# The opening of a two-layer backbone kernel, up to group 0's first eight tiles, issued in written order on four engines

## The chip, the cores and the metric

The kernel runs on one core of a Trainium2 chip. The metric is device time in microseconds (us) of one launch. The engines are PE (TensorE, matrix multiply), DVE (VectorE), ACT (ScalarE), POOL (GpSimd) and SP (SyncE, which here issues all loads).

## The reference, cut to what matters

Four mixers exist; two layers are run, so only the pooling mixer (layer 0) and the neighbourhood attention (layer 1) occur. What follows is layer 0, on 256 latent and 256 context tokens of width 2048:

```
ml = (silu(c) @ w_mod[i] + b_mod[i]).reshape(B, 6, 1, D)       # 6 x 2048 modulation values, and the same for c_ctx
a  = rms_norm(h, norm1_g) * (1 + scale) + shift                # ml[:,1], ml[:,0]
h  = h + ml[:, 2] * pool_mix(a, pool_w, pool_b, pool_scale)    # 4 groups of 512 channels, windows 2/4/8/16
u  = rms_norm(h, norm2_g) * (1 + ml[:, 4]) + ml[:, 3]
h  = h + ml[:, 5] * conv_ffn(u, w_gate, w_up, ...)             # 2048 -> 5504 (gate, up) -> 2048
```

`pool_mix` takes a windowed mean minus the token itself, and multiplies each group of 512 channels by its own 512 x 512 matrix.

## The kernel before, in words

All products that need single precision are made of three fast ones: a weight and an activation are split into a high part (a cast on ACT, line 152 for weights) and a low part (a subtraction on DVE, line 155), and hi x hi, hi x lo and lo x hi are added up in PSUM.

The 24 chunks of 512 modulation values are made in **modulation steps** (`mod_pe`, line 189; matmuls at line 197). A chunk has four steps. One step loads 1 MB of `w_mod` in two loads of 512 KB and multiplies it in four column blocks of 32, two blocks from each load; line 197 has eight PE instructions for a step and four for a half. After the fourth step of a chunk comes its finish: ACT copies the sum out (line 204), PE transposes it four times (line 209), DVE reduces it and adds bias and gain (lines 213, 178, 180). The generator `pump0` runs steps in the order of chunks 4, 0, 8, 16, 12, and then two at a time; `need(n)` advances it to step n.

Layer 0's mixer and the first half of its feed-forward are interleaved by groups of 512 channels. `mixer(0)` (from line 627) makes the pooled values of group 0 (`pfs`), scales them by chunk 4 (line 663), shifts them by chunk 0 (line 664), splits them (`parts_of`, lines 614 and 615), multiplies them by `wp[0]` into four banks `pm0_0` to `pm0_3` (`pool_mm`, lines 623, 624, 626), scales the result by chunk 8 (`gsc`, `gbi`, lines 691 and 693; 707 and 710) and adds it to the streams `hl` and `hc` (line 712). Then it scales these by chunk 16 into the split operands `Ad` (lines 722, 723). `partial(0)` multiplies `Ad` by the first eight blocks of `w_gate` and `w_up`: a **tile** is twelve matmuls (lines 787 to 789) into one bank, four tiles come from one pair of loads (`wcg`, `wcu`), and each sum is copied out (line 799). `early_shifts` (line 743) multiplies the same raw weight loads by chunk 12, which DVE has copied into `sh` (line 573).

Loads go to 15 **rooms** of 512 KB that are used in turn (`stage`, line 117): six in the pool `wst` and the unused operand rooms A7 to A15 (nine, given by `lend`). A room is free again when the last instruction that reads it is done.

The order of instructions on each engine is chosen by the framework's planner, which goes by the order of the code, by what its own plan says is ready, and by a few marks: `tc.high_priority()`, `tc.issue_after(ins)`. So two halves of one step can stand apart on PE, with other matmuls between them, and a load can be issued ahead of an earlier one whose room isn't free.

Of the kernel before, what the change touches and what calls it, by code (L numbers as in the profile page):

```python
# [17 lines left out]
P = 128  # L18
D = 2048
KT = D // P  # L20
T = 256
# [39 lines left out]
def kernel(ctx: ExitStack, tc: tile.TileContext, xT, cxT, wmod, wg, wu, wd, wp,  # L61
# [20 lines left out]


# [26 lines left out]
    made = []  # L110
    first_split = []
# [28 lines left out]
    def split(ts, name, share=0, lows=None):  # L140

        parts = []
        for j, (t, n) in enumerate(ts):
# [5 lines left out]
            with ExitStack() as behind:  # L149
                for ins in hold:  # L150
                    behind.enter_context(tc.issue_after(ins))
                cast = nc.scalar.copy(hi[:, :n], t[:, :n])  # L152
                eng = nc.gpsimd if share and turn[0] % share == 0 else nc.vector
                if lows is None:
                    low = eng.tensor_tensor(lo[:, :n], t[:, :n], hi[:, :n].bitcast(F32), op=ALU.subtract)  # L155
                    made[:] = [cast.ins, low.ins]
                else:
                    lows.append((lo, t, hi))
# [27 lines left out]
    def behind(ch, j):  # L186
        return tc.issue_after(first_split[j]) if ch == 16 else ExitStack()

    def mod_pe(chs, sc, pool):

        ps = bank("m", f"mod{chs[0]}")
        for c, ch in enumerate(chs):
            for g in range(4):
# [7 lines left out]
                if ch == chs[-1] and g == 3:  # L201
                    ev = pool.tile([P, 512], F32, tag="t2", name=f"modev{ch}")
                    with tc.high_priority() if ch in (0, 4, 8, 16) else ExitStack(), behind(ch, 0):
                        copied[ch] = nc.scalar.copy(ev, ps).ins
                yield
        with tc.high_priority() if ch in (0, 4, 8, 16) else ExitStack():
# [3 lines left out]
            for c, ch in enumerate(chs):  # L210
                r = main.tile([P, 4, 2], F32, name=f"modT0_{ch}")
                with behind(ch, 1):
                    nc.vector.tensor_reduce(out=r, in_=by_row(p2, 2 * c), axis=AX.X, op=ALU.add)
                finish_mod(0, ch, r)

# [258 lines left out]
    with ExitStack() as ph0:  # L474
# [58 lines left out]
        with ExitStack() as phs:  # L533
# [50 lines left out]
            def need(n):  # L584
                while done[0] < n:
                    next(pump0, None)
                    done[0] += 1
# [40 lines left out]
            def mixer(g):  # L628
# [8 lines left out]
                if g == 0:  # L637
# [19 lines left out]
                    parts = split(load(lambda a, b: wp[0][:, a:b], 2048, "wp0"), "wp0", lows=lows)  # L657
                    yield
                    for k in range(4):
                        for s in both:  # L660
                            v = pfs[k][:, s, :]
                            with tc.issue_after(copied[0]) if k > 1 else ExitStack():
                                nc.scalar.activation(v, v, AF.Copy, scale=M(0, 1, k, s))
                            nc.vector.scalar_tensor_tensor(v, z, M(0, 0, k, s), v, op0=ALU.mult, op1=ALU.add)
# [4 lines left out]
                    yield  # L669
# [21 lines left out]
                nc.vector.tensor_tensor(gsc, modT[0, 8 + g].rearrange("p i s -> p (i s)"), V("ps")[:, 8 * g : 8 * g + 8],  # L691
                                        op=ALU.mult)
                nc.vector.tensor_tensor(gbi, gsc, V("pb")[:, 8 * g : 8 * g + 8], op=ALU.mult)
                for m in range(4):
                    if banks:
                        ps = banks[m]
                    else:
                        ps = bank("d", f"pm{g}_{m}")
                        for i in range(4):
                            pool_mm(ps, parts, pa, i, m)  # L700
                    k = 4 * g + m
                    y = f0.tile([P, 2, T], F32, tag="t2", name=f"pz{k}")
                    for s in both:
                        j = 2 * m + s
                        v = ps[:, T * s : T * s + T]
                        if g == 0 and s == 0:
                            nc.vector.tensor_scalar(y[:, s], v, gsc[:, j : j + 1], gbi[:, j : j + 1],
                                                    op0=ALU.mult, op1=ALU.add)
                        else:
                            nc.scalar.activation(y[:, s], v, AF.Identity, scale=gsc[:, j : j + 1], bias=gbi[:, j : j + 1])  # L710
                        eng = nc.vector if g == 0 and s == 0 else nc.gpsimd
                        eng.tensor_tensor(h_of(s)[:, k, :], h_of(s)[:, k, :], y[:, s], op=ALU.add)
                    if g:
                        n2.add(h_of, k)
# [3 lines left out]
                for i in range(4):  # L718
# [8 lines left out]
                    if i == 1:  # L727
# [25 lines left out]

            def partial(g, sh, between):
# [3 lines left out]
                for fa in range(0, NS, 4):  # L758
                    for q, (nm, wsrc) in enumerate((("g", wg), ("u", wu))):
                        if step:  # L760
                            ahead.clear()
                        if ahead:
                            ts, parts = ahead
                        else:
                            ts = load(lambda a, b: wsrc[0, fa + a // 512 : fa + b // 512, :, 512 * g : 512 * g + 512]
                                      .rearrange("f p c -> p f c"), 2048, f"wc{nm}{g}_{fa}")
                            parts = split(ts, f"wc{nm}{g}_{fa}")
                        for j in range(4):
# [14 lines left out]
                            hi, lo = parts[j // 2]  # L783
                            for i in range(4):
                                o = 512 * (j % 2) + P * i
                                xh, xl = flat(A[4 * g + i][:, 0]), flat(A[4 * g + i][:, 1])
                                nc.tensor.matmul(ps, hi[:, o : o + P], xh, start=(first and i == 0), stop=False)
                                nc.tensor.matmul(ps, hi[:, o : o + P], xl, start=False, stop=False)
                                ins = nc.tensor.matmul(ps, lo[:, o : o + P], xh, start=False, stop=(final and i == 3))
                                if i == 1:  # L790
                                    between(2 * step + 1)
                            step += 1
                            first_tile.append(ins.ins)
                            if f >= NC:
                                continue
                            if g == 0:
                                if q == 0:
                                    PART[f] = act_tile(f"part{f}", F32)
                                nc.scalar.copy(PART[f][:, q], ps)
                            else:  # L800
                                ins = nc.vector.tensor_tensor(PART[f][:, q], PART[f][:, q], ps, op=ALU.add)
                                if g == 3:
                                    added.append(ins.ins)
# [11 lines left out]
            first_tile = []  # L815
            first = mix = mixer(0)
            for n in (0, 8, 11, 13, 13, 17, 17):
                if n == 17 and not ahead:
                    need(15)
                    ahead.append(load(lambda a, b: wg[0, 0:2, :, 0:512].rearrange("f p c -> p f c"), 1024, "wcg0_0"))  # L820
                    ahead.append(split(ahead[0], "wcg0_0"))
                    first_split[:] = made
# [785 lines left out]
```

## Time and profile before

| | us |
|---|---|
| median of 3 runs (lowest, highest) | 3010.19 (3008.44, 3012.23) |
| the profiled execution, its own time | 3006.95 |
| span of the profile | 3005.2 |
| PE busy in the span | 2954.4 (98%) |
| DVE, ACT, POOL busy | 2035.4, 1353.9, 876.8 |

Times in the profile count from the start of the span. A matmul's end is modelled, so pitches between starts say more than durations. "xN" is a number of instructions; the bracket behind a row is the idle time before it on its engine and what ended it.

### The profile page before, as it was taken

Reading aid. Unit: us, or ns where it says so; the run is one execution under the profiler, and the core shown is the slowest. Engines: PE = TensorE matmul, PEld = TensorE weight load, DVE = VectorE, ACT = ScalarE, POOL = GpSimd, SP = SyncE. Lnnn points to the kernel's source line nnn. Section 1 sums busy time; section 2 is a strip of 40 time slices with the busy share of each in tenths; the row PEclk is TensorE's granted clock in tenths of the full one; section 3 lists DMA queues with packets and bytes.
Section 4 is the critical chain, followed back from the end, with each engine's and each line's share of the span. In section 5 each row is a group of like instructions: output and inputs, shape, how many; then the busy total and the mean of one; then the engine's idle time right before and its main releaser. Section 6 shows DMA issues by size and latency. Waiting matters only on the chain.

```text
span 3005.2 us, 41071 instructions
## 1 busy us (share of the span) xinstructions
PE 2954.4 (98%) x14922; PEld 2402.8 (80%) x14922; DVE 2035.4 (68%) x2908; ACT 1353.9 (45%) x2225; POOL 876.8 (29%) x864
## 2 busy tenths in 40 slices
PE   7999999999999999999999999999999999999998
PEld 3655678888888888888887888888888888888887
DVE  5455887666786867688777656474877666666666
ACT  3333573323333233333434434353556666566665
POOL 1011310312214031231422111020101565566665
PEclk9999999999999999999999999999999999999999
DMA  9988535555876867786782333333356565555553
GB/s 390 344 297 324 198 99 177 166 174 169 247 209 185 269 181 234 211 246 192 229 242 85 123 107 113 97 118 95 118 165 207 170 203 194 189 180 187 185 187 113
DMA packets 224923, 572.32 MB, mean 190 GB/s; under 512 B 55248, under 2 KB 68304, under 8 KB 224720
## 3 DMA queue, kind: packets, MB, share of 16 engines
q1 hardware_dynamic: 224720, 569.70, 58.6%
q8 instruction: 117, 1.92, 0.3%
q14 instruction: 86, 0.70, 0.1%
HBM read 563.32 MB, written 11.53 MB: 191 GB/s over the span
## 4 chain that ended last, share of the span: by engine, by line
PE 93%; DVE 3%; DMA 2%; ACT 1%; issue 1%; POOL 0%; SPq 0%; DVEq 0%; ACTq 0%; POOLq 0%
PE g L1102 5%; PE u L1102 5%; PE d L950 5%; PE d L952 5%; PE d L951 5%; PE d L1174 5%; PE u L915 4%; PE u L913 4%; PE u L914 4%; PE g L915 4%; PE g L914 4%; PE g L913 4%; PE u L1109 3%; PE g L1109 3%; PE d L1178 3%; PE mod L197 2%
## 5 line engine op out<-in xcount | busy, mean ns | idle before, releaser
L971 POOL TENSOR_TENSOR hl<-hl,dy 128x256 f32<-128x256 f32 x144 | 148.7, 1033 | 921.4 <-ACT dy L968 662.2
L1191 POOL TENSOR_TENSOR hl<-hl,dy 128x256 f32<-128x256 f32 x320 | 313.6, 1011 | 231.6 <-ACT dy L1189 228.7
L284 DVE SCALAR_TENSOR_TENSOR macc<-wm,sc,macc 128x512 f32<-128x512 f32 x360 | 262.8, 780 | 7.7 <-DMA wm<-wmod 7.4
L262 DVE SCALAR_TENSOR_TENSOR macc<-wm,sc,macc 128x1024 f32<-128x1024 f32 x120 | 161.3, 1344 | 91.9 <-DMA wm<-wmod 90.9
L968 ACT ACTIVATE dy<-d,modT 128x256 f32<-128x256 f32 x224 | 93.2, 470 | 121.0 <-PE d L952 114.9
L971 POOL TENSOR_TENSOR hc<-hc,dy 128x256 f32<-128x256 f32 x144 | 141.8, 985 | 0.0
L1372 POOL COPY bias<-rows 128x160 f32<-128x160 f32 x64 | 39.7, 631 | 312.7 <-DVE nm L1381 234.5
L1189 ACT ACTIVATE dy<-d,modT 128x512 f32<-128x512 f32 x160 | 104.6, 684 | 57.1 <-PE d L1178 55.5
L155 DVE TENSOR_TENSOR wd_3l<-wd,wd_3h 128x1024 fp32r<-128x1024 f32 (+1 forms) x44 | 56.0, 1278 | 79.6 <-ACT wd_3h L152 79.0
L517 ACT ACTIVATE sg<-g 128x512 f32<-128x512 f32 x43 | 27.3, 634 | 160.1 <-DVE g L514 160.0
L197 PE MATMUL mod<-wm,sc 128*32 128x512 f32 x640 | 95.3, 606 | 3.1 <-DMA wm<-wmod 2.9
L155 DVE TENSOR_TENSOR wd_2l<-wd,wd_2h 128x1024 fp32r<-128x1024 f32 (+1 forms) x44 | 58.2, 1333 | 41.9 <-ACT wd_2h L152 41.4
L607 POOL TENSOR_TENSOR pf<-ws,inv 128x256 f32<-128x256 f32 x32 | 29.3, 937 | 195.8 <-DVE ws L599 86.2
L155 DVE TENSOR_TENSOR wd_1l<-wd,wd_1h 128x1024 fp32r<-128x1024 f32 (+1 forms) x44 | 55.2, 1259 | 36.7 <-ACT wd_1h L152 36.7
L152 ACT CAST wd_0h<-wd 128x1024 fp32r<-128x1024 f32 (+1 forms) x44 | 45.2, 1031 | 57.9 <-PE g L914 41.1
L152 ACT CAST wd_1h<-wd 128x1024 fp32r<-128x1024 f32 (+1 forms) x44 | 44.9, 1029 | 51.8 <-PE u L1102 28.8
L950 PE MATMUL d<-act,wd_0h 128*128 128x512 f32 x172 | 66.4, 390 | 1.0 <-ACT dy L968 1.0
L950 PE MATMUL d<-act,wd_3h 128*128 128x512 f32 x172 | 67.2, 391 | 0.0
L952 PE MATMUL d<-act,wd_2l 128*128 128x512 f32 x172 | 67.2, 390 | 0.0
L951 PE MATMUL d<-act,wd_2h 128*128 128x512 f32 x172 | 67.1, 390 | 0.0
L950 PE MATMUL d<-act,wd_2h 128*128 128x512 f32 x172 | 66.9, 389 | 0.0
L952 PE MATMUL d<-act,wd_0l 128*128 128x512 f32 x172 | 66.9, 389 | 0.0
(1710 smaller groups left out, 9319.6 us busy)
## 6 DMA issues: line engine op xcount, KB each, us to landing
wm<-wmod SPq DMA_DIRECT2D x384, 512.0 KB, 6.2
wd<-wd SPq DMA_DIRECT2D x168, 512.0 KB, 4.4
wg<-wg SPq DMA_DIRECT2D x156, 512.0 KB, 4.5
wu<-wu SPq DMA_DIRECT2D x156, 512.0 KB, 4.7
wv<-wv SPq DMA_DIRECT2D x32, 512.0 KB, 3.9
wk<-wq SPq DMA_DIRECT2D x32, 512.0 KB, 3.8
wq<-wq SPq DMA_DIRECT2D x32, 512.0 KB, 3.7
wo<-wo SPq DMA_DIRECT2D x32, 512.0 KB, 4.2
```

The lines of the kernel that those rows point to most:

```text
L155: low = eng.tensor_tensor(lo[:, :n], t[:, :n], hi[:, :n].bitcast(F32), op=ALU.subtract)
L284: nc.vector.scalar_tensor_tensor(acc[:, s], w, sc2[:, k, s : s + 1], acc[:, s], op0=ALU.mult, op1=ALU.add)
L913: nc.tensor.matmul(ps, hi[:, c : c + P], xh, start=(k == 0), stop=False)
L914: nc.tensor.matmul(ps, hi[:, c : c + P], xl, start=False, stop=False)
L915: nc.tensor.matmul(ps, lo[:, c : c + P], xh, start=False, stop=(k == KT - 1))
L950: nc.tensor.matmul(ps, hi[:, o : o + P], xh, start=(i == 0), stop=False)
L951: nc.tensor.matmul(ps, hi[:, o : o + P], xl, start=False, stop=False)
L952: nc.tensor.matmul(ps, lo[:, o : o + P], xh, start=False, stop=(i == n - 1))
L971: nc.gpsimd.tensor_tensor(h_of(s)[:, k, :], h_of(s)[:, k, :], y[:, s], op=ALU.add)
L1102: ins = nc.tensor.matmul(ps, hi[:, c : c + P], flat(x[k]), start=(k == 0), stop=False)
L1109: nc.tensor.matmul(ps[:, T:], lo[:, c : c + P], x[k][:, 0], start=False, stop=(k == KT - 1))
L1191: nc.gpsimd.tensor_tensor(hl[:, k, :], hl[:, k, :], y[:, q], op=ALU.add)
```

## The change

A helper `written()` takes every instruction that is traced in its block on PE, ACT, DVE and SP, and makes each follow the one before it on its engine, so that each of these engines runs the block in the order of the code. POOL is left out. The block holds the opening from chunk 0's finish to the eighth tile of group 0, and its code is written out anew: modulation steps stand whole, between groups of `pm` matmuls and between tiles; the finish of chunks 0, 8 and 16 is a step of its own of the generator, which `finish()` takes; the four results of the mixer are scaled and added one by one (`mixed(m)`); chunk 16 is finished ahead of the low half of the first gate weights. Two tiles start together (`opening`), the order of the three kinds of products is hi-hi, lo-hi, hi-lo there, and the loads of `wcu` stand behind step 20. The sums of squares of group 0 (`n2.add`) come behind the block. The marks `behind`, `hold` and `first_split` around this stretch go away. The core of the diff:

```diff
+    @contextmanager
+    def written():
+        traced = nc.cur_bb.bb.instructions
+        last = traced[-1]
+        yield
+        at = next(k for k in reversed(range(len(traced))) if traced[k] is last) + 1
+        before = {}
+        for i in traced[at:]:
+            if i.engine not in (nc.tensor.engine, nc.scalar.engine, nc.vector.engine, nc.sync.engine):
+                continue
+            if i.engine in before:
+                tc.add_manual_dep(i, before[i.engine].name, ..., reason="written order")
+            before[i.engine] = i
...
                 finish_mod(0, ch, r)
+        if chs[-1] in (0, 8, 16):
+            yield "finished"
...
+                    parts = split(ts[:1], "wp0_0", lows=lows)
                     for k in range(4):
                         for s in both:
                             v = pfs[k][:, s, :]
-                            with tc.issue_after(copied[0]) if k > 1 else ExitStack():
-                                nc.scalar.activation(v, v, AF.Copy, scale=M(0, 1, k, s))
                             nc.vector.scalar_tensor_tensor(v, z, M(0, 0, k, s), v, op0=ALU.mult, op1=ALU.add)
                         pa.append(parts_of(pfs[k], k))
-                    with tc.issue_after(low_done[-1]):
-                        for lo, t, hi in lows:
-                            nc.vector.tensor_tensor(lo, t, hi.bitcast(F32), op=ALU.subtract)
-                    yield
+                        if k == 1:
+                            parts += split(ts[1:], "wp0_1", lows=lows)
+                    for lo, t, hi in lows:
+                        nc.vector.tensor_tensor(lo, t, hi.bitcast(F32), op=ALU.subtract)
                     banks = [bank("gu", f"pm0_{m}") for m in range(4)]
                     for i in range(4):
-                        for m in range(4):
-                            pool_mm(banks[m], parts, pa, i, m, (True, False))
-                    for i in range(4):
-                        for m in range(4):
+                        if i != 1:
+                            need(9 + max(0, i - 1))
+                        for j in range(2):
+                            for m in range(4):
+                                c = 512 * (i % 2) + P * m
+                                nc.tensor.matmul(banks[m], parts[i // 2][0][:, c : c + P], flat(pa[i][:, j]), ...)
+                    need(12)
...
+                    rest_of(0)
+                    finish()
+                    nc.vector.tensor_tensor(gsc, flat(modT[0, 8]), V("ps")[:, 0:8], op=ALU.mult)
+                    nc.vector.tensor_tensor(gbi, gsc, V("pb")[:, 0:8], op=ALU.mult)
+                    mixed(0)
+                    need(14)
+                    rest_of(1)
+                    mixed(1)
+                    need(15)
+                    rest_of(2)
+                    mixed(2)
+                    need(16)
+                    ahead.append(load(lambda a, b: wg[0, 0:2, ...], 1024, "wcg0_0"))
+                    lows = []
+                    ahead.append(split(ahead[0], "wcg0_0", lows=lows))
+                    ahead[0] += load(lambda a, b: wg[0, 2:4, ...], 1024, "wcg0_1")
+                    rest_of(3, range(2))
+                    finish()
+                    for lo, t, hi in lows:
+                        nc.vector.tensor_tensor(lo, t, hi.bitcast(F32), op=ALU.subtract)
+                    rest_of(3, range(2, 4))
+                    mixed(3)
...
+            def opening():
+                ts, parts = ahead
+                hi, lo = zip(*parts)
+                banks = [bank("d", f"cg0_{j}") for j in range(2)]
+                for i in range(4):
+                    xh, xl = flat(A[i][:, 0]), flat(A[i][:, 1])
+                    for w, x in ((hi, xh), (lo, xh), (hi, xl)):
+                        for j in range(2):
+                            products(banks[j], w, x, j, i, ...)
+                for j in range(2):
+                    put(banks[j], 0, 0, j)
+                need(18)
+                for j in range(2, 4):
+                    ps = bank("d", f"cg0_{j}")
+                    tile_of(ps, parts, 0, j, True, True)
+                    put(ps, 0, 0, j)
+                    if j == 2:
+                        need(20)
+                        us = load(lambda a, b: wu[0, ...], 2048, "wcu0_0")
+                        uparts = split(us, "wcu0_0")
+                for j in range(4):
+                    need(21 + 2 * j)
+                    if j < 2:
+                        early_shifts(0, j, shs[0], (ts, us)[j])
+                    ps = bank("d", f"cu0_{j}")
+                    tile_of(ps, uparts, 0, j, True, True)
+                    put(ps, 0, 1, j)
...
-            for n in (0, 8, 11, 13, 13, 17, 17):
-                if n == 17 and not ahead:
-                    need(15)
-                    ahead.append(load(...)); ahead.append(split(ahead[0], "wcg0_0"))
-                    first_split[:] = made
+            for n in (0, 8):
                 need(n)
-                if n == 17 and len(ahead[0]) == 1:
-                    ahead[0] += load(lambda a, b: wg[0, 2:4, ...], 1024, "wcg0_1")
                 next(mix)
-            hold[:] = [copied[16], low_done[-1]]
-            ahead[1] += split(ahead[0][1:], "wcg0_1")
-            hold.clear()
+            with written():
+                finish()
+                next(mix)
+                ahead[1] += split(ahead[0][1:], "wcg0_1")
+                opening()
+            next(first)
```

## Rows read from the trace of the kernel before

**Rows 1.** The page: busy share of the DMA engines in tenths, 40 slices.
```profile
DMA  9988535555876867786782333333356565555553
```

**Rows 2.** Windows: stretch and length, busy of five engines, clock, DMA share, GB/s.
```profile
8.00:82.00 74.00, 62.01 (x292) 28.80 (x292) 40.17 (x78) 29.02 (x67) 11.53 (x13) 0.98 1.02 407
...
111.40:336.00 224.60, 221.57 (x1246) 134.87 (x1246) 132.22 (x214) 79.80 (x143) 41.52 (x48) 1.00 0.81 299
```

**Rows 3.** Timeline, PE: start, length, work, count, [idle before, what ended it].
```profile
41.64 1.05 PE L197 MATMUL mod<-wm,sc 128*32 128x512 f32 x4 [1.39 <-DMA wm<-wmod]
...
50.32 0.39 PE L623 MATMUL pm<-ph,wp0h 128*128 128x512 f32 x1
50.55 0.39 PE L624 MATMUL pm<-ph,wp0h 128*128 128x512 f32 x1
50.87 1.05 PE L197 MATMUL mod<-wm,sc 128*32 128x512 f32 x4
51.85 0.50 PE L623 MATMUL pm<-ph,wp0h 128*128 128x512 f32 x1
...
63.70 3.64 PE L197 MATMUL mod<-wm,sc 128*32 128x512 f32 x32
```

**Rows 4.** Timeline, PE: early shifts; a whole step between matmuls; behind the eighth tile.
```profile
86.93 1.08 PE L743 MATMUL pw<-wcg,sh 128*32 128x256 f32 x16
...
108.50 0.39 PE L789 MATMUL cu<-Ad,wcu_0l 128*128 128x512 f32 x1
108.81 1.06 PE L197 MATMUL mod<-wm,sc 128*32 128x512 f32 x8
109.81 0.50 PE L787 MATMUL cu<-Ad,wcu_0h 128*128 128x512 f32 x1
...
111.40 1.09 PE L743 MATMUL pw<-wcg,sh 128*32 128x256 f32 x16
```

**Rows 5.** Timeline, DVE, ACT and POOL: the mixer's operands, its result, chunk 16's finish.
```profile
40.80 3.25 DVE L664 SCALAR_TENSOR_TENSOR pf<-z,modT,pf 128x256 f32<-128x256 f32 x8
...
43.04 2.18 ACT L614 CAST ph<-pf 128x512 fp32r<-128x512 f32 x4
...
43.98 2.49 DVE L615 TENSOR_TENSOR ph<-pf,ph 128x512 fp32r<-128x512 f32 x4
...
65.94 3.33 POOL L712 TENSOR_TENSOR hc<-hc,pz 128x256 f32<-128x256 f32 x4 [26.35 <-ACT pz L710]
...
68.05 0.60 ACT L204 COPY modev<-mod 128x512 f32<-128x512 f32 x1
...
70.61 0.18 DVE L213 TENSOR_REDUCE modT<-modt 128x8 f32<-128x32 f32 x1
```

**Rows 6.** The chain that ended last, 64 to 73: start, length, engine and line.
```profile
64.63 1.90 DVE pz L707 x4
...
66.88 2.68 DVE hl L712 x3
69.56 1.13 DVE wcg_0l L155
71.29 0.92 ACT Ad L722 x2
72.25 0.73 PE cg L787 x2
```

**Rows 7.** Timeline, SP, 70 to 100: issues of loads.
```profile
70.70 0.38 SPq L136 DMA_DIRECT2D wcu<-wu  x1
78.63 9.78 SPq L136 DMA_DIRECT2D wm<-wmod  x9
88.52 0.39 SPq L136 DMA_DIRECT2D wcu<-wu  x1
90.16 9.57 SPq L136 DMA_DIRECT2D wm<-wmod  x2
```

**Rows 8.** The loads of `wmod` up to 160: time from issue to landing.
```profile
DMA to landing us min/median/max: 3.9/9.1/11.7
```

More of the change, by code (lines that the diff above doesn't have):

```diff
@@ L674, in mixer @@
[L674 to L676 removed]
+                        if i != 1:
[3 more added lines that the diff above has]
+                                c = 512 * (i % 2) + P * m
+                                nc.tensor.matmul(banks[m], parts[i // 2][0][:, c : c + P], flat(pa[i][:, j]),
+                                                 start=(i == 0 and j == 0), stop=False)
@@ new lines, in mixer, with rest_of, mixed @@
+                    need(12)
+                    def rest_of(m, ks=range(4)):
+                        for i in ks:
+                            pool_mm(banks[m], parts, pa, i, m, (False, True))
+                    def mixed(m):
+                        y = f0.tile([P, 2, T], F32, tag="t2", name=f"pz{m}")
+                        for s in both:
+                            j = 2 * m + s
+                            v = banks[m][:, T * s : T * s + T]
+                            if s == 0 and m < 3:
+                                nc.vector.tensor_scalar(y[:, s], v, gsc[:, j : j + 1], gbi[:, j : j + 1],
+                                                        op0=ALU.mult, op1=ALU.add)
+                            else:
+                                nc.scalar.activation(y[:, s], v, AF.Identity, scale=gsc[:, j : j + 1],
+                                                     bias=gbi[:, j : j + 1])
+                            eng = nc.vector if s == 0 and m < 3 else nc.gpsimd
+                            eng.tensor_tensor(h_of(s)[:, m, :], h_of(s)[:, m, :], y[:, s], op=ALU.add)
@@ L752, in early_shifts, with products, tile_of @@
                 nc.vector.tensor_tensor(sums[0], old, pw, op=ALU.add)
+            def products(ps, w, x, j, i, first, final):
+                o = 512 * (j % 2) + P * i
+                return nc.tensor.matmul(ps, w[j // 2][:, o : o + P], x, start=first, stop=final).ins
+            def tile_of(ps, parts, g, j, first, final, between=None):
+                hi, lo = zip(*parts)
+                for i in range(4):
+                    xh, xl = flat(A[4 * g + i][:, 0]), flat(A[4 * g + i][:, 1])
+                    products(ps, hi, xh, j, i, first and i == 0, False)
+                    products(ps, hi, xl, j, i, False, False)
+                    products(ps, lo, xh, j, i, False, final and i == 3)
+                    if i == 1 and between is not None:
+                        between()
@@ new lines, in put @@
+            def put(ps, g, q, f):
+                if g == 0:
+                    if q == 0:
+                        PART[f] = act_tile(f"part{f}", F32)
+                    nc.scalar.copy(PART[f][:, q], ps)
+                else:
+                    ins = nc.vector.tensor_tensor(PART[f][:, q], PART[f][:, q], ps, op=ALU.add)
+                    if g == 3:
+                        added.append(ins.ins)
+            def opening():
+                ts, parts = ahead
+                hi, lo = zip(*parts)
+                banks = [bank("d", f"cg0_{j}") for j in range(2)]
+                for i in range(4):
+                    xh, xl = flat(A[i][:, 0]), flat(A[i][:, 1])
+                    for w, x in ((hi, xh), (lo, xh), (hi, xl)):
+                        for j in range(2):
+                            products(banks[j], w, x, j, i, i == 0 and w is hi and x is xh, i == 3 and x is xl)
+                for j in range(2):
[7 more added lines that the diff above has]
+                        need(20)
+                        us = load(lambda a, b: wu[0, a // 512 : b // 512, :, 0:512].rearrange("f p c -> p f c"), 2048, "wcu0_0")
+                        uparts = split(us, "wcu0_0")
[6 more added lines that the diff above has]
+                    put(ps, 0, 1, j)
@@ L782, in partial @@
                                 first = final = True
[L783 to L791, printed above, removed]
-                            step += 1
[L793 to L803, printed above, removed]
+                            tile_of(ps, parts, g, j, first, final, lambda: between(2 * step + 1))
+                            step += 1
+                            if f < NC:
+                                put(ps, g, q, f)
                         c += 1
```

89 lines of the change are left out of this document (37 added, 52 removed).

## The prediction

> **What bounds the kernel now.** PE is busy for 98% of the span, so away from the opening a change is worth the PE time that it saves. I read three views of the opening. The DMA share by slices says that the first two slices (150 us) are the ones that are nearly full [rows 1]; by windows the loads run at 407 GB/s from 8 to 82 us, and at 299 GB/s from 111 to 336 [rows 2]. So up to about 82 us data can arrive no sooner; at that rate a 512 KB load takes 1.25 us. The timeline of PE shows what PE makes of the data: modulation steps as halves of four instructions between other matmuls [rows 3]. The chain of waits leaves PE for DVE and ACT from 64 to 72 us, just ahead of the first tile [rows 6]. I compare both kernels at one place: 28 steps, eight tiles and chunk 12 done, where PE starts the shifts of the second gate weights. That is 111.40 us before [rows 4].
>
> **Prices.** A matmul of 512 columns follows another after 0.23 us (50.32 to 50.55 [rows 3]), and twelve make a tile of 2.75. A half step in a stream of matmuls takes 51.85 - 50.55 - 0.23 = 1.07 [rows 3]; a whole step takes 109.81 - 108.50 - 0.23 = 1.08 [rows 4]. So a half costs as much as a whole: its column blocks run beside each other, and two alone take as long as four. Further whole steps in a row cost (3.64 - 1.06) / 3 = 0.86 each [rows 3]. Early shifts take 1.05 [rows 4].
>
> **Steps 9 to 16 and the mixer's matmuls.** Nothing moves up to chunk 0's finish. Load 17 of `wmod` lands at 41.6 [rows 3]; from there load n in the new order (step 9 to 16, two gate loads, step 17 to 20, two `wcu`, step 21 on) lands 1.25 later each: step 12 at 50.4, step 16 at 60.4, step 20 at 72.9, step 21 at 77.9. Of its 48 mixer matmuls and eight steps, before runs four steps as eight halves between 41.6 and 60 (all eight visits look like the one in [rows 3]), which are 8 x 1.07 where four whole ones cost 4 x 1.08: 4.3 us, but the first waits for its load in either kernel.
> New order on PE: step 9 ends at 43.8 (its second half lands at 42.9). Two groups of eight matmuls (1.83 each): 47.5. Step 10, a group, step 11, a group, step 12: 54.4. Is it fed? DVE and ACT now take turns for each of the four values: two shifts (0.41 each), ACT's cast (0.55), DVE's low part (0.62) [rows 5], with handovers 2.1 us; the low parts stand at 43.4 (one weight cast comes first), 45.4, 47.5 and 49.5, and PE asks for them at 44.7, 46.6, 49.5 and 52.4. So this slower order is hidden by PE, with 0.8 us to spare at the least; if that cover were gone, each us would go on the path. Four low matmuls (0.9), chunk 8's transposes (0.6), steps 13 and 14 (1.94), four, step 15, four, step 16: 61.8, each step landed before it is asked for. Before, step 16 ends at 63.70 + 3.64 = 67.3 [rows 3]. **Gain so far 5.5 us.**
>
> **From step 16 to the first tile.** Before needs 72.25 - 67.3 = 4.9 us: DVE has scaled (1.90), added (2.68) and made the gate weights' low half (1.13) before it reduces chunk 16 [rows 6]. Now three of four results are mixed earlier, and that low half stands behind the finish. New: ACT copies the sum out (0.60), four transposes (0.6), reduce, bias and gain (from 70.61 to ACT's start at 71.29, 0.7) [rows 5, 6]: 63.9. But ACT has the two halves of result 3 first (0.5 each) and then two `Ad` casts (71.29 on, 0.4 to 0.5 each): 65.8. POOL's two additions for result 3 (0.83 each [rows 5]) end at 66.2, and `Ad` 3 is cast at 67.4 at the earliest, in time. So 4.0 us in place of 4.9; **gain 6.4 us**, PE idle for 2.
>
> **The tiles.** 24 matmuls (5.5): 71.3. Steps 17, 18: 73.2; tile: 75.9; 19, 20 (landed at 72.9): 77.9; tile: 80.6; transposes and step 21: 82.3. The shifts wait for `sh`: DVE has the two low halves of `wcu` before it, which follow ACT's copy of chunk 12 and two casts, and is through at about 82.7. Shifts 83.7, tile 86.5.
> Here **the change adds a wait.** SP too runs in written order. The two gate loads sit in rooms 35 and 36 of the count until the shifts have read them. The pools of these rooms (two in one, one in the other) come round at loads 50 and 51, the second half of step 22 and the first of step 23. Load 49 is in at 79.1; load 50 can't be issued before 83.7, and everything behind it on SP waits too, with idle DMA engines. Before, the planner issued loads for other rooms ahead of blocked ones, and it still has such pauses: nothing from 71 to 78.6, nothing from about 91 to 99 [rows 7]; the second `wcu` load goes out at 88.5, right behind the shifts of 86.93 [rows 4, 7]. A load into an idle queue lands no sooner than 3.9 us after issue (the least of 86; the median is 9.1 with a full queue) [rows 8]. So load 50 lands at 87.7, and load 52 at 90.2 to 91.5; I take 90.9. Step 23 then ends at 91.9 in place of 88.4. Shifts and tile: 95.6; steps 24, 25: 97.6; tile: 100.3; 26, 27: 102.3; tile: 105.0. Step 28 asks for load 64, twelve loads or 15 us after load 52, at 105.9, and ends at 106.9.
> The Trainium skill speaks against this part (DMA: Bandwidth & Descriptors, "Anatomy of one DMA"): a DMA engine waits for no semaphore, the issuing sequencer does, ahead of dispatch. The pauses of [rows 7] agree. [...]
> The same page's "Specifications" set 358 GB/s as what HBM gives one core; an estimate by it lands step 16 at 63.6 rather than 60.4 and takes some 2 us off the gain. The windows show 407 [rows 2], so the sum doesn't go by it.
>
> **Sum.** 106.9 against 111.40: 4.5 us less. Bounds of the opening: 2.5 (the restart takes 2 us longer, or ACT and DVE queue up once more ahead of the first tile) to 8.8 (no restart: step 23 ends at 88.4 and step 28 at 102.6). Behind it the work is the same: 111.40 to 336 ran at 299 GB/s [rows 2], under what the engines moved before, so 4.5 us less lead can be made up, and PE keeps the gain to the end. The eight additions to the second norm's sum go behind the block, where DVE is busy for 132 of 225 us [rows 2]; I cost them at nothing; as much as 3 us if PE had to wait for them, which it does only in group 3. The profiled execution is 3006.95, its span 3005.2, the median of the runs 3.2 above it at 3010.19: 3006.95 - 4.5 = 3002.4, and for the median **3005.7**.
>
> **Rivals.**
> - *The wait on SP does not come.* If the planner's rooms fall otherwise, or DVE's `sh` is early, the opening keeps 8.8 us: 3001.4. For it: PE could do it; against it: the same room wait shows before, at 88.5 [rows 7]. 0.18.
> - *Given back.* The planner orders all the rest anew; before has hardly a wait in that stretch (221.6 of 224.6 us busy [rows 2]), so a new order has more to lose than to win. A loss of about 4 ends near 3010. 0.20.
> - *Slower: broken steps behind the block.* The block leaves loads no lead: load 64 lands after it is asked for. Where the planner finds only one half of a step landed, it may start it alone, as it did eight times between 41.6 and 60 [rows 3]. Each such half costs 1.07 - 0.43 = 0.64 more, a pair with its own return to the matmuls 1.07. Fifty-two steps follow. From four broken steps on the gain is gone; ten cost 10.7 and give 3016.4. Against it: DMA has a fifth to spare there [rows 2]. 0.12.
> - *The order does not hold*, since the helper's links reach only instructions of the block and others may be put between: then a part of the halves stays, and the time lies between no change and my forecast. It is in the second rival's share.
>
> **How the numbers follow.** Forecast, opening gains 2.5 to 6.5 and keeps it, 3003.5 to 3008: 0.50; no SP wait 0.18; given back 0.20; slower 0.12. A difference under 0.2%, 6 us, can hardly be told from none here. Faster by more than that: the first rival and the forecast's upper end, 0.18 + 0.09 = 0.27. Slower by more: 0.11 (ten broken steps or more). Within: 0.62. The range that leaves out 2 in 10 runs from the first rival's 3001.4 less 1.5 for its own bound to about half of the slower rival, 3000 to 3013.
>
> **What would show it.** PE in the new trace: no group of four at line 197 from 43 to 107; step 16 ended at 61.8; first `cg` matmul at 65.8; a pause of SP from about 80 to 83.7 and PE waiting for `wm` at 86 to 91; the shifts of the second gate weights at 106.9. It would be wrong if PE waited for `ph` or low parts of `wp` between 44 and 55, if the `Ad` casts were later than 66, or if groups of four at line 197 came up in number behind 107.

## The result and the profile after

The changed kernel takes 3015.88 us (median of 17 runs, 3014.03 to 3020.25) against 3009.04 of the kernel before beside it (17 runs): ratio 1.0023, 95% interval 1.0016 to 1.0031. It is 6.8 us slower; 3005.7 was forecast, and the time lies above the range of the forecast. The profiled execution's span is 3015.2, ten more than before's 3005.2.

Windows of the kernel after (columns as in [rows 2]; the first and third answer those rows):
```profile
8.00:82.00 74.00, 62.30 (x307) 30.92 (x308) 39.13 (x76) 30.89 (x70) 12.44 (x14) 0.95 0.97 394
82.00:111.40 29.40, 25.13 (x133) 13.44 (x132) 8.44 (x12) 9.07 (x18) 0.00 (x0) 0.94 0.83 317
111.40:336.00 224.60, 222.19 (x1213) 131.11 (x1213) 125.93 (x206) 71.65 (x124) 34.61 (x40) 1.00 0.82 299
```
The loads of the first 82 us move at 394 GB/s in place of 407, the clock is below 1.00, and from 82 to 111.4 PE is idle for 4.3 us. Timeline of PE (start, length, work, count, [idle before, what ended it]):
```profile
42.46 2.18 PE L207 MATMUL mod<-wm,sc 128*32 128x512 f32 x8 [1.33 <-DMA wm<-wmod]
...
62.18 1.06 PE L207 MATMUL mod<-wm,sc 128*32 128x512 f32 x8
...
67.12 0.73 PE L809 MATMUL cg<-Ad,wcg_0h 128*128 128x512 f32 x2 [1.96 <-ACT Ad L775]
...
68.26 1.95 PE L809 MATMUL cg<-Ad,wcg_0h 128*128 128x512 f32 x4
...
74.64 1.92 PE L207 MATMUL mod<-wm,sc 128*32 128x512 f32 x16
...
87.08 1.10 PE L796 MATMUL pw<-wcg,sh 128*32 128x256 f32 x16 [1.25 <-DVE sh L584]
...
91.05 1.05 PE L207 MATMUL mod<-wm,sc 128*32 128x512 f32 x4
95.12 3.65 PE L207 MATMUL mod<-wm,sc 128*32 128x512 f32 x10 [3.02 <-DMA wm<-wmod]
...
103.26 1.91 PE L207 MATMUL mod<-wm,sc 128*32 128x512 f32 x12
105.10 1.21 PE L809 MATMUL cg<-Ad,wcg_4h 128*128 128x512 f32 x4
106.24 1.05 PE L207 MATMUL mod<-wm,sc 128*32 128x512 f32 x4
...
112.22 1.05 PE L207 MATMUL mod<-wm,sc 128*32 128x512 f32 x4
...
114.33 1.05 PE L207 MATMUL mod<-wm,sc 128*32 128x512 f32 x4
...
122.24 1.09 PE L796 MATMUL pw<-wcg,sh 128*32 128x256 f32 x16
```
The opening does what it says up to 84: whole steps (x8, x16), step 16 at 62.18 where before ran its last steps from 63.70 [rows 3], first gate matmul at 67.12 where before had 72.25 [rows 6]. Then PE waits for `sh`, waits for a load, and from 103 on steps are broken again: x12 is step 24 and the first half of step 25, and x4 a half. Twelve halves stand apart between 103 and 157, the six pairs of chunks 5 and 17. Three of these pairs, steps 25 to 27, belong to the written block; between their halves run matmuls of the next gate weights (`wcg_4`), which do not. So the links keep the block's instructions in order, but they don't keep others out. At the point of comparison, 122.24 against 111.40 [rows 4], 24 matmuls of the next gate weights lie inside (24 x 0.23 = 5.5) and one step less (1.07): 122.24 - 5.5 + 1.07 = 117.8, so 6.4 late where 4.5 early was forecast.

The chain of the kernel after, 80 to 96 (start, length, what):
```profile
82.01 1.06 ACT wcu_0h L166
...
84.23 1.22 DVE wcu_0l L169
85.45 0.10 DVE modT L222
85.55 0.60 DVE n2acc L378
86.15 0.09 DVE modT L191
86.24 0.02 issue
86.25 0.69 DVE n2acc L378
86.95 0.09 DVE sh L584
87.04 0.04 issue
87.08 1.17 PE pw L796 x16
88.25 6.83 DMA wm<-wmod
95.08 0.04 issue
95.12 3.65 PE mod L207 x10
```
Two additions for the second norm (line 378) stand between DVE's reduce of chunk 12 and its copy into `sh`; the shifts follow; load 50 goes out right behind the shifts, at 88.25, and lands 6.83 later. SP's timeline:
```profile
67.75 2.81 SPq L150 DMA_DIRECT2D wm<-wmod  x3
85.86 0.89 SPq L150 DMA_DIRECT2D wcg<-wg  x2
88.25 11.10 SPq L150 DMA_DIRECT2D wm<-wmod  x12
```
and SP's waits from 70 to 100 (us in total, times, longest):
```profile
SPq L150 <- DMA wm<-wmod: 12.7, 6, 7.2
SPq L150 <- PE mod L207: 8.1, 1, 8.1
SPq L150 <- PE pw L796: 1.4, 1, 1.4
```
SP issues nothing from 70.6 to 85.9. At the head of its queue stand the next gate weights (`wcg_4`), which are not in the block and come behind all its loads in the code: the first waits 7.2 us for a load of `wmod` to land and then 8.1 us for step 21, which reads that room and ends at 85.8. Load 50 then waits 1.4 for the shifts, as forecast. Windows show the cost, and one more loss, the clock:
```profile
68.00:70.00 2.00, 2.00 (x6) 1.38 (x5) 2.00 (x6) 2.00 (x5) 0.00 (x0) 0.61 1.02 418
70.00:72.00 2.00, 2.00 (x6) 1.57 (x5) 1.72 (x3) 0.40 (x1) 0.00 (x0) 0.54 1.03 417
82.00:84.00 2.00, 2.00 (x11) 1.60 (x9) 0.91 (x1) 2.00 (x4) 0.00 (x0) 1.00 0.00 0
```
From 82 to 84 the DMA engines move nothing. From 68 to 72 the granted clock is near its lower level (1.2 of 2.4 GHz), after PE was idle for 1.96 us.

### The profile page after: what moved, and what is told of

It is laid out like the page before. It is cut to its first block, busy times and chain, and to the rows that moved or that the text cites. A ratio compares the mean times of both kernels' runs of the same rounds, so it can differ in the third digit from the quotient of the medians.

```text
span 3015.2 us, 41074 instructions
## 1 busy us (share of the span) xinstructions
PE 2960.5 (98%) x14922; PEld 2403.5 (80%) x14922; DVE 2035.6 (68%) x2906; ACT 1355.4 (45%) x2226; POOL 875.3 (29%) x865
## 3 DMA queue, kind: packets, MB, share of 16 engines
q8 instruction: 117, 1.92, 0.3%
## 4 chain that ended last, share of the span: by engine, by line
PE 88%; DVE 5%; DMA 3%; issue 3%; ACT 1%; POOL 0%; SPq 0%; DVEq 0%; ACTq 0%; POOLq 0%
PE g L1181 5%; PE u L1181 5%; PE d L1031 5%; PE d L1029 5%; PE d L1030 5%; PE d L1253 5%; PE u L994 4%; PE u L993 4%; PE u L992 4%; PE g L994 4%; PE g L993 4%; PE g L992 4%; PE u L1188 3%; PE g L1188 3%; PE d L1257 3%
## 5 line engine op out<-in xcount | busy, mean ns | idle before, releaser
L1031 PE MATMUL d<-act,wd_1l 128*128 128x512 f32 x172 | 67.0, 390 | 0.1
L166 ACT CAST wd_3h<-wd 128x1024 fp32r<-128x1024 f32 (+1 forms) x44 | 45.3, 1031 | 48.7 <-PE u L1181 31.9
```

## The experiments

Two theories. **Queue** (A in the recorded texts): the time goes where loads wait for rooms in SP's written order. **Halves** (C): the block moves the broken steps out of chunk 8 into chunks 5 and 17, where PE has nothing to wait for. B there is the low clock. Each kernel has 9 or 11 runs, with 15 to 33 of the kernel before beside it. "Lag" in the texts is the start of the n-th recorded PE matmul less that of the kernel before; orders differ, so it tells a few us, not tenths. "Halves apart" are counted in the order on PE: 20 before, 20 after.

**e1_sp_free.** SP is left out of the written order.
```
-   if i.engine not in (tensor, scalar, vector, nc.sync.engine): continue
+   if i.engine not in (tensor, scalar, vector): continue
```


> The changed kernel with SP taken out of the written order; PE, ACT and DVE keep it. Theory A (SP's written order lets one blocked load empty the DMA queue, and all later losses follow from the lost lead): the pause in landings from 80 to 90 us shrinks to under 4 us, the broken steps behind the block become fewer, and of the 6.8 us that the change lost some 4 to 6 come back: ratio to the kernel before 1.0003 to 1.0010. Theory B (the half clock and PE's waits inside the block cost it, SP has no part): within 0.0005 of 1.0023. Theory C (the planner breaks steps behind the block whatever the loads do): also near 1.0023, with as many halves apart as the changed kernel has.


Measured: 1.0016 (1.0007 to 1.0025), above the 1.0003 to 1.0010 of theory A. What comes back, 0.0007, is less than the uncertainty of the difference. The window of 80 to 88 shows that the pause of the DMA engines is nevertheless gone:
```profile
80.00:88.00 8.00, 7.97 (x48) 4.29 (x46) 2.75 (x4) 4.90 (x11) 0.00 (x0) 1.00 0.98 358
```
PE still waits 5.0 us for loads of `wmod` between 62 and 102 (3.0 in the changed kernel): SP waits for the same rooms, now behind other loads. So the pause alone is not what the change lost.

**e5_rooms.** From the second gate load to the block's end the two rooms that the shifts hold are not used.
```
+   for r in ("wm", "wa"): rooms.remove(r)      # behind the load of wcg0_1
    ...
+   rooms[:0] = ["wm", "wa"]                    # behind the block
```


> The changed kernel with the written order on all four engines, but the two rooms of the first gate weights left out of turn until the block ends (13 rooms in turn instead of 15), so that loads 50 and 51 need not wait for the shifts of chunk 12. Theory A: landings go on from 80 to 90, PE's wait from 92 to 95 and the slow clock behind it go, the eight tiles end some 6 us earlier than in the changed kernel, ratio 0.9995 to 1.0008. Theory B: only the first slow stretch matters, ratio 1.0018 to 1.0025. Theory C: the opening gets faster but broken steps behind the block take it again: 1.0010 to 1.0020.


Measured: 1.0017 (1.0008 to 1.0025). The engines move 399 GB/s from 80 to 88, PE has no wait at 91 to 95, and at 400 matmuls (100 us) the lag is about -5 in place of +2: the opening's gain is there, and it is gone again by 172, as theory C had it. Broken halves come at 136 and 138, and at the hand-over to group 1 ACT stands in the way (ACT's timeline, then PE's):
```profile
160.48 1.04 ACT L166 CAST wcu_0h<-wcu 128x1024 fp32r<-128x1024 f32 x1 [1.43 <-DMA wcu<-wu]
...
161.75 0.49 ACT L777 ACTIVATE Ad<-hl,modT 128x256 fp32r<-128x256 f32 x1
...
162.69 0.73 PE L811 MATMUL cg<-Ad,wcg_0h 128*128 128x512 f32 x2 [2.11 <-ACT Ad L777]
```
ACT's cast of a weight waits for its load, and the `Ad` casts that PE needs are queued behind it.

**e4_warm.** Eight matmuls into an unused bank fill PE's idle time ahead of the first tile; nothing else uses them.
```
+   fill = bank("d", "fill")                    # behind rest_of(3, range(2, 4))
+   for _ in range(8): nc.tensor.matmul(fill, parts[0][0][:, 0:P], flat(pa[0][:, 0]), start=True, stop=True)
```


> The changed kernel with eight extra matmuls of 512 columns (1.8 us) into a bank that nobody reads, where PE stands idle ahead of the first tile (65.2 to 67.1). The kernel's own work is unchanged. Theory B: the granted clock stays at its upper level between 68 and 72 (0.5 to 0.6 in the changed kernel), the 24 matmuls there take 5.5 instead of 7.5 us, and 2 us or more stay to the end: ratio 1.0012 to 1.0017. Theory A: the opening gets 2 us earlier, but the load that waits for the shifts of chunk 12 still lands 10 us behind the last one, so the broken steps stay and about 2 us stay as well: 1.0015 to 1.0023. If the clock falls nevertheless, the idle time ahead of the tile wasn't its cause.


Measured: 1.0025 (1.0016 to 1.0035). The clock from 64 to 72 is 1.00, and the end doesn't move. But the first tile starts 2.1 us later than in the changed kernel (67.12), so that behind its 24 matmuls the two stand level (74.64 there):
```profile
69.19 0.73 PE L812 MATMUL cg<-Ad,wcg_0h 128*128 128x512 f32 x2 [1.05 <-ACT Ad L778]
...
74.84 1.92 PE L207 MATMUL mod<-wm,sc 128*32 128x512 f32 x16
```
Then `sh` comes later still (PE waits 2.9 us for it), and the clock falls at 88. So e4 doesn't price the slow matmuls. That they are not what sets the end is seen in e14 below, the fastest kernel: its clock is 0.69 from 68 to 72.

**e3_before_whole.** The kernel before with each step's second pair of columns first.
```
-   for j in range(4):
+   for j in (2, 3, 0, 1):
```


> The kernel before with one edit: a step multiplies the blocks of its second load first, so that the planner has no reason to start it before both loads are in. It leaves everything else to the planner. If a half costs what a whole step costs, the eight halves between 41 and 60 become four whole steps and up to 4.3 us go there, less what PE then waits for loads: ratio 0.9985 to 0.9995. Rival: PE waits for the same loads either way, or the planner's new order costs as much elsewhere: 0.9995 to 1.0010.


Measured: 0.9989 (0.9980 to 0.9998). Thirteen halves stand apart, none of them between 41 and 60, and at 300 matmuls (84 us) the lag is only about -1. That speaks for eight halves of chunk 8 that lie mostly beside the chain of DVE and ACT ahead of the gate; e15 below doesn't bear it out.

**e2, e6, e7, e8: whole steps everywhere.** The same edit and high priority for the second pair, in the changed kernel (e2), in e5 (e6), in e1 (e7) and in the kernel before (e8).
```
-   for j in range(4):
-       nc.tensor.matmul(...)
+   for j in (2, 3, 0, 1):
+       with tc.high_priority() if j < 2 else ExitStack():
+           nc.tensor.matmul(...)
```


> The changed kernel with each modulation step behind the opening issued as whole (its second pair of columns right behind its first, the pair after that under high priority), so that the broken halves of chunks 5 and 17 are mostly gone: 10 halves stand apart in the order on TensorE in place of 20. Theory C (the broken halves, moved from chunk 8 into chunks 5 and 17 by the block, cost about 0.64 us each of the loss): 10 x 0.5 to 0.64 = 5 to 6 us come back, 3010 to 3011.5 us, ratio 1.0004 to 1.0012. Theory A (the loads that can't be issued from 80 to 86 and the hand-over to group 1 set the end, the halves lie beside them): within 1 us of the changed kernel, ratio 1.0020 to 1.0026.

> e5_rooms (loads of the opening wait for no room by name) with whole steps behind the block: 8 halves stand apart in place of 15. Theory C: the 5 us of the opening are kept up to the hand-over to group 1 and the halves' 7 x 0.64 = 4.5 us don't come: lag at 750 matmul records 0 or below, end about 3005 to 3008 us, ratio 0.9988 to 1.0000. Rival: the hand-over to group 1 (ScalarE's cast of the first gate weights ahead of the casts that the first gate matmul needs, 162 to 166 us) takes what the opening gave, whole steps or not: 3011 to 3013, ratio 1.0008 to 1.0014.

> e1_sp_free (SyncE's part of the opening isn't in the written order) with whole steps behind the block: 4 halves stand apart in place of 11. Theory C: 7 x 0.64 = 4.5 us back from 3014: about 3009.5, ratio 0.9998 to 1.0010. Rival (hand-over to group 1 sets it): ratio 1.0012 to 1.0018, as e1.

> The kernel before with whole steps (as e3, the second pair now also with the priority): 9 halves stand apart in place of 20. If halves cost 0.3 us each, as e3's 3.5 us for 7 fewer would have it at 0.5: 11 x 0.3 to 0.5 = 3 to 5.5 us, 3003.5 to 3006, ratio 0.9982 to 0.9990. Rival (the chain of VectorE and ScalarE ahead of the gate bounds the opening and the halves lie beside it): 3005 to 3009, ratio 0.9989 to 1.0000.


Measured: e2 1.0021 (1.0012 to 1.0029), e6 0.9989 (0.9980 to 0.9998), e7 1.0003 (0.9995 to 1.0012), e8 0.9981 (0.9973 to 0.9990). e2 came out where theory A had it, e6 and e7 where theory C had it: alone the edit brings nothing, with free rooms it brings 0.0028 (e5 to e6). With whole steps everywhere the written block brings nothing either: with free rooms (e6) it is 0.0008, 2.4 us, slower than no block (e8), less than the uncertainty. e2 has a loss of its own, though. Windows from 36 to 48, first of the kernel after:
```profile
36.00:40.00 4.00, 3.16 (x12) 0.43 (x12) 2.71 (x3) 1.12 (x4) 3.05 (x4) 1.00 1.03 421
40.00:44.00 4.00, 2.12 (x10) 0.74 (x12) 1.73 (x5) 3.48 (x7) 0.00 (x0) 1.00 1.03 420
44.00:48.00 4.00, 4.00 (x19) 2.85 (x16) 2.63 (x7) 2.19 (x3) 0.00 (x0) 1.00 1.03 416
```
and of e2:
```profile
36.00:40.00 4.00, 1.29 (x12) 0.16 (x8) 3.96 (x7) 2.58 (x5) 2.07 (x4) 1.00 1.03 416
40.00:44.00 4.00, 1.92 (x12) 0.65 (x12) 2.69 (x7) 1.99 (x6) 2.15 (x3) 0.65 1.02 417
44.00:48.00 4.00, 3.18 (x10) 1.97 (x7) 2.63 (x6) 2.05 (x5) 0.00 (x0) 0.50 1.03 419
```
With whole steps in chunks 4 and 0, PE waits for both loads of a step and is busy for 1.29 and 1.92 of 4 us; then the clock falls to its lower level and the mixer's matmuls run slow. So e2 changed two things.

**e13, e14, e15, e16: whole steps from step 21 on.** Chunks 0, 4, 8, 12 and 16 as they were (steps 21 to 27 still belong to the block): e13 is the changed kernel, e14 is e5, e15 the kernel before, e16 is e12 (below) with this edit.
```
+   late = chs[-1] not in (0, 4, 8, 12, 16)
+   for j in (2, 3, 0, 1) if late else range(4):
+       with tc.high_priority() if late and j < 2 else ExitStack():
```


> The changed kernel with whole steps only behind the opening (chunks 4, 0, 8, 16 and 12 issued as in the changed kernel): 12 halves stand apart in place of 20. Theory (the halves behind the block cost about 0.6 us each, and e2 lost this gain again by the low clock from 40 to 56 us, which cost it 3.7 us at 200 matmul records): no low clock at 40 to 56, 3010.5 to 3012.5 us, ratio 1.0005 to 1.0012. Rival (the wait for loads hides the halves, as e2 seemed to say): 1.0018 to 1.0025.

> e6_rooms_whole with whole steps only behind the opening. Theory of the low clock: e6 without its spell at 40 to 48 us, 1 to 3 us better than 0.9989: 0.9979 to 0.9986. Rival (the spell is hidden behind the loads, which set the opening to step 16): 0.9987 to 0.9993, as e6.

> The kernel before with whole steps only behind the opening; the eight halves of chunk 8 between 41 and 60 us stay apart. Theory (the eight halves are hidden behind the chain of VectorE and ScalarE ahead of the gate, and whole steps there only bring the low clock of 40 to 56 us): as good as or better than e8, 0.9972 to 0.9984. Rival (the eight halves are what e3 and e8 gained by): 0.9990 to 1.0000.

> e12_n2_inside with whole steps only behind the opening: the opening in written order, no waits for rooms, second norm's squares behind the first shifts, no low clock at 40 to 56. Theory: 1 to 3 us better than e12's 0.9983: 0.9973 to 0.9981. If it is not below e15 by more than 0.001, the written order of the opening brings nothing that whole steps behind it don't bring without it.


Measured: e13 1.0007 (0.9998 to 1.0015), e14 0.9975 (0.9965 to 0.9985), e15 0.9991 (0.9982 to 0.9999), e16 0.9981 (0.9972 to 0.9989). In e13 the clock is 1.00 from 40 to 56 and 12 halves stand apart; 4.8 us come back, and eight fewer at the predicted 0.64 are 5.1. e15 came out as its rival had it: e8, which has chunk 8 whole too, is at 0.9981. The eight halves of chunk 8 may be worth something after all, but the difference, 0.0010, is less than its uncertainty. e14 has the lowest time, 3002.86 us (2999.24 to 3004.74), faster than both kernels, though not told apart from e16, nor from e8 and e11, which have no block. Up to 159 us e14 and e5 have the same lag; at 167, past the hand-over to group 1, e5 is 4 us later than e14, and at 211 it is 10. e16 lies 0.0010 below e15; its text asked for more than that before the written order counts as worth anything. What the rooms do is seen in the windows 80 to 96, first of e13:
```profile
80.00:88.00 8.00, 6.75 (x47) 4.32 (x47) 5.29 (x9) 5.41 (x12) 0.00 (x0) 1.00 0.26 82
88.00:96.00 8.00, 3.22 (x20) 1.33 (x22) 1.23 (x1) 2.02 (x3) 0.00 (x0) 0.82 0.98 334
```
then of e14:
```profile
80.00:88.00 8.00, 6.72 (x48) 4.05 (x45) 5.30 (x9) 5.99 (x13) 0.00 (x0) 1.00 1.00 379
88.00:96.00 8.00, 8.00 (x58) 4.80 (x60) 0.69 (x1) 0.64 (x2) 0.00 (x0) 1.00 0.93 309
```
PE's wait falls due some 8 us after the engines stood still: 4.8 us of idle PE in the second window of e13, none in e14.

**e9, e10, e12: the second norm behind the shifts.** In e9 (from e6) and e10 (from e5) `n2.add` is issued behind the copy into `sh`; that moved DVE's additions, but ACT's squares kept their place between the two casts of `wcu_0`. In e12 (from e6) the whole of it is written into the block.
```
+   with tc.issue_after(shifted[0]) if not g else ExitStack():   # e9, e10, around n2.add
+   if j == 0: next(first)                # e12, in opening() behind early_shifts; not behind the block
```


> e6_rooms_whole with the squares and sums of group 0's second norm set behind the copy of the shift coefficients: in e6 the gate's shifts waited 2.92 us for that copy (88.22 us), since ScalarE squared from 82.66 to 86.0 between the two casts of wcu_0. Theory: the second cast follows the first, the copy comes at about 85, the shifts start at about 85.6 in place of 88.45, and if no other loss takes the place 1.5 to 2.9 us are kept to the end: 3002.5 to 3004, ratio 0.9979 to 0.9984. Rival (given back behind the opening, at the hand-over to group 1, as the other gains of the opening were): 0.9986 to 0.9992.

> e5_rooms (no load of the opening waits for a room by name, steps behind the block still broken) with the squares and sums of group 0's second norm behind the copy of the shift coefficients. In e5 the shifts waited 1.3 us for that copy. Theory: lag at 350 to 400 matmul records 1 us better than e5's -4.2 and -5.3. If the broken steps behind the block set the loss, the end stays at 1.0010 to 1.0017; if the hand-over to group 1 does (ScalarE's queue), a different order there may move it by 2 to 4 us either way.

> e6_rooms_whole with the squares and sums of group 0's second norm written into the opening, behind the copy of the first shifts, so that ScalarE's two casts of wcu_0 stand together (in e9 only VectorE's sums had moved; the squares still stood between the casts, and the shifts started only 0.6 us earlier). The shifts of the first gate weights should start at about 85.6 to 86 in place of 88.45, their wait 0 to 0.5 in place of 2.92. Theory (what the opening gains is kept where nothing else is late): 2 to 2.9 us to the end, 3002.5 to 3003.5, ratio 0.9979 to 0.9983, as good as whole steps without the written order (0.9981). Rival (given back behind the opening): 0.9987 to 0.9993, as e6 and e9.


Measured: e9 0.9991 (0.9982 to 1.0000), e10 1.0009 (1.0000 to 1.0018), e12 0.9983 (0.9974 to 0.9992). PE's waits from 82 to 100, in e6 and then in e12:
```profile
PE pw L799 <- DVE sh L585: 2.9, 1, 2.9
```
```profile
PE pw L799 <- DVE sh L585: 0.2, 1, 0.2
```
The wait goes and 0.0006 is left of it at the end, less than the intervals; between e14 and e16 it has the other sign. So the second norm, in the queues of ACT and DVE, explains when the shifts start, not the time. e9 came out as its rival had it, given back behind the opening.

**e11_before_whole_again.** The program of e8 once more.


> The same program as e8_before_whole2 (the kernel before, whole modulation steps, no written order), beside e9 on the same chip: 0.9973 to 0.9990 again. If e9 is not below it by more than 0.001, the written order of the opening brings nothing beyond what whole steps bring without it.


Measured: 0.9981 (0.9972 to 0.9990), as e8. e9, with the block, lies 0.0010 above it, not below: by the text's own measure the written order brings nothing there beyond what whole steps bring alone.

Together, as ratios to the kernel before (each 0.0009 wide to either side, a difference of two some 0.0013, 4 us):
```
                                steps broken   whole everywhere   whole from step 21 on
no block (the kernel before)    1              0.9981 (e8, e11)   0.9991 (e15)
block, as changed               1.0023         1.0021 (e2)        1.0007 (e13)
block, SP free                  1.0016 (e1)    1.0003 (e7)        not run
block, two rooms left out       1.0017 (e5)    0.9989 (e6)        0.9975 (e14)
```
In the last column the parts come apart. The block with free rooms against no block, e15 to e14: 4.8 us faster. The room wait, e14 to e13: 9.6 us slower. The halves: 4.8 us in the changed kernel, 2.7 in the kernel before. So -4.8 + 9.6 + (4.8 - 2.7) = +6.9, which adds up in any case, since it goes round the table; what the runs show are the single steps. The first of them holds in this column alone: in the middle one the same step, e8 to e6, goes 2.4 us the other way, and the lowest time with the block (e14) is 1.8 below the lowest without (e8, e11), within the uncertainty. Taken in the other order the shares differ: with broken steps the rooms are worth 1.8 us (e5), and the halves then 12.6. The two together cost the changed kernel 14.4 us either way; how they split depends on which is taken first. The rest of the order changes with each edit, too, and that each sets the next wait where the other is gone is likely but not shown.

## Why the prediction was wrong, step by step

- **Prices.** Right: two whole steps 1.92 for 1.94, a half 1.05, early shifts 1.10. One side estimate is mis-added: with step 16 landing at 63.6 it would end near 64.5 in place of 61.8, and 2.7 us go off the gain, not 2. The sum doesn't use it.
- **Step 16.** It ends at 62.18 + 1.06 = 63.2, not 61.8; 0.8 of the 1.4 is there at step 9, which ends at 44.6 for 43.8, behind its load. No wait for `ph` or low parts followed, so the slower operand order was hidden, as argued. Gain 4.1, not 5.5.
- **First tile.** 67.12 for 65.8, idle 1.96 for 2: the step was right and carries the 1.3 on (so the `Ad` casts start at 66.17, past the 66 named as a sign of being wrong). Not in the sum: the 24 matmuls take 7.5 for 5.5 at the low clock. What this costs at the end no run shows alone (e4 starts its tile later); e14, too, has slow matmuls there, and the lowest time.
- **`sh` and the eight additions.** "I cost them at nothing" looked at PE behind the block alone. Two of them stand in front of `sh`; the shifts start 1.25 behind step 21 where 0.4 was expected. Again small in the end (e12, e16).
- **The wait on SP.** The mechanism was right: load 50 can't go out before the shifts have run, the DMA engines stand idle, PE then waits for `wm` and the clock falls behind it. For most of the time it is `wcg_4` that holds the head of the queue, but load 50, too, had to wait for the shifts. The size failed, in three terms. The shifts came 4.4 us later than put (87.08 for 82.7), the issue 4.6 (88.25 for 83.7). The load took 6.83 from issue to landing, not 4.0, as two loads of `wcg_4` went ahead of it, which the sum didn't have in this stretch. And with the engines idle from 80 to 86, the loads had no lead left for what follows (in e1 they aren't idle, and PE waits all the same). The sum gave this wait 8.8 - 4.5 = 4.3 us; e13 to e14 shows 9.6. The first of the two `wcg_4` loads landed 4.2 us after its issue into idle engines, near the least of [rows 8], 3.9. The Trainium skill's rule that the issuing sequencer, not the DMA engine, waits (DMA: Bandwidth & Descriptors, "Anatomy of one DMA") agrees with SP's waits above.
- **"Behind it the work is the same."** This is the step that failed besides. The slower rival, broken steps behind the block, got 0.12 on the ground that DMA has a fifth to spare there. It came: six pairs, three of them inside the stretch that was summed and inside the block, where the code has whole steps. A share of DMA over 225 us says nothing of the lead at one step; it was lost by 86 us. The rival said that four pairs eat the gain and ten give 3016.4; six came, and e13, with eight halves fewer, gave 4.8 us back. With the 9.6 - 4.3 = 5.3 of the wait this is 10.1 of the 11.3 us between 4.5 faster and 6.8 slower, if the parts are taken in that order.
- **"The order does not hold."** This rival, which got no chance of its own, came in part: matmuls of `wcg_4` broke steps 25 to 27, and the loads of `wcg_4` went ahead of load 50. The sum counted the latter at their place in the code, behind the block's loads. No run ties them down, so their own cost stays open.
- **The opening itself.** Freed of both, the block is worth 4.8 us against e15, inside the 2.5 to 8.8 that bounded it; in the column with whole steps everywhere it brings nothing (e8 to e6). That it is worth anything in general is not shown.
- **Given back** (0.20) was right in kind too: in e5 the opening's 5 us are gone behind the hand-over to group 1.

## What to carry to other kernels

When part of a program is fixed in written order, ask whether instructions from outside can still be put between. Look at what is at the head of the loading engine's queue at every point of it, with loads from outside the part too, and ask which reader frees that room and when: one blocked load stops all, and its price falls due microseconds later. Count the lead that the loads have at the end of the fixed part; where there is none, a planner starts work on halves. And try two suspected causes together as well as singly: here either edit alone brought 5 us at most, and the two 14.

## What the runs showed of the hardware

Two of a step's four column blocks take as long on PE as all four (1.05 and 1.06 us), so a broken step costs nearly twice a whole one. An idle PE of 1.96 us ahead of the first tile was followed by a granted clock of 0.54 to 0.61 from 68 to 72 in the kernel after and of 1.00 in e5 and e13; e8 and e11, the same program, differ too (0.79 and 1.00 from 72 to 80), so such a fall isn't a property of the program alone. From 40 to 48 the clock was 0.50 to 0.57 in all eight profiles of kernels with whole steps everywhere (e3 among them), 0.79 in e5 and e10, and 1.00 in the others; ahead of it, where it fell, PE waits for loads, as e2's windows show. Behind the idle stretch of the DMA engines, 80 to 86, a load of 512 KB landed 4.2 us after its issue; one that was issued behind two such loads took 6.83.
